# An MoE kernel: the last expert's products in high and low parts, and the gates' transposes in another place of the order

## Chip, core and metric

One core of one Trainium2 chip runs the whole program in one launch. The metric is the device time of an execution in microseconds (us); the kernel is run several times and the median is taken. One execution is also profiled: its span is the time from the first to the last instruction, and the profile's rows are measured from the span's start.

## What is computed

The program is a two-layer backbone over 256 latent tokens and 256 context tokens of width 1024 (fp32 everywhere): a recurrent mixer in layer 0, a short gated convolution in layer 1, and behind each a mixture of 16 experts, of which every token uses two. The change lies in the experts alone:

```python
combine = jnp.einsum('nk,nke->ne', gate, jax.nn.one_hot(experts, N_EXPERTS))
out = jnp.zeros_like(hf)
for e in range(N_EXPERTS):
    he = jax.nn.silu(hf @ w_gate[e]) * (hf @ w_up[e])     # 1024 -> 512, twice
    out = out + combine[:, e:e + 1] * (he @ w_down[e])    # 512 -> 1024
```

The reference computes every expert on every token; `combine` is zero where a token doesn't use the expert, so the kernel gathers only the tokens that do.

## The kernel before

`moe` runs once in each layer. The router gives each token its rank among the tokens of each of its experts. An expert has a fixed number of slots: 64 (`SL`) for experts 0 to 14, 128 for expert 15. If an expert got more tokens than slots, a branch behind expert 12 (`OVER`, the `If` at L1724) computes the rest; with this data the branch isn't taken, but every engine has to arrive at it.

What is done for one expert e, with the names of its tiles:

- **gather** (L1500, matmuls L1510, tile `xeps`): the columns of the normed tokens `h2t` are multiplied with a one-hot matrix `g`, for all experts of a group at once. The groups are experts 0-3, 4-7, 8-11, 12-14, and 15 alone; the gather of the next group is cut in four pieces, and one piece is issued in each iteration. ScalarE (L1519) and VectorE (L1516) evict the pieces into `xe`, with the layer's scale and shift.
- **gate_up** (L1548, matmuls L1558, tile `wup`): `xe` is the stationary operand, the weights `w` move through, 512 columns at a time. Eight blocks of the 1024 inputs, two matmuls each, for the gate and the up half. With 64 slots the two halves go to partitions 0-63 and 64-127, and the two matmuls of a block run side by side in the array. ScalarE (silu) and VectorE (product) make `sgate` of it.
- **turn** (L1566, transposes L1571, tile `hetp`): `sgate` is transposed; ScalarE copies it to `het`. It stands in the middle of the next expert's gate_up.
- **down** (L1576, matmuls L1585, tile `y`): four blocks, two matmuls each. ScalarE (L1596) and VectorE (L1597) evict `y` times the gate into `yy`, the one the positive part, the other what is left of it.
- **gates** (L1489, tile `gps`): two transposes of the one-hot matrix (L1493) and two one-column matmuls that pick the gate weights (L1495). ScalarE copies the transposes to `st` (L1497), VectorE the weights to `gw` (L1498).
- **scatter** (L1600, matmuls L1605, tile `acc`): `yy` is multiplied with `st` and added to the layer's output in PSUM.

In iteration e the program is written in the order gate_up(e), with turn(e - 1) in its middle; scatter(e - 2); down(e - 1); gates(e); one piece of the next group's gather. For expert 15 turn(14) stands ahead of its gate_up. A scheduler moves the instructions of an engine against each other within what their data allow, so the order on TensorE is not the written one.

All matmuls of gate_up and down are fp32, which TensorE executes as two passes: the trace has two rows for one such matmul. Gather and scatter are fp32r, a form with fewer bits that takes one pass. A layer's projections (L142 to L144, with the splits at L1105 and L1108) get fp32 accuracy with fp32r in another way: each operand is split in a high part (a cast to fp32r) and a low part (what is left), and three of the four products are added: high x high, low x high, high x low.

`gps`, `xeps` and `y` share a PSUM pool of two buffers (`psy`); `wup` and `hetp` have another. The weights come through a ring of eleven 1 MB tiles (`w`), six to an expert, on the queue of SyncE (L163): the next tile is asked for as soon as one is let go of.

Of the kernel before, what the change touches and what calls it, by code (L numbers as in the profile page):

```python
# [21 lines left out]
P = 128  # L22
# [107 lines left out]
class Kern:  # L130
# [1321 lines left out]
    def moe(self, l, h, ro, then):  # L1452
# [4 lines left out]
        with ExitStack() as outer:  # L1457
# [12 lines left out]
            pool = es.enter_context(tc.tile_pool(name="mo", bufs=2))  # L1470
            acc = [t[:, f] for t in [psa.tile([P, NB // 2, T], F32, name=f"acc{i}") for i in range(2)]
# [28 lines left out]
            def gather(g, ne, n, xe, step=2, turns=(psy, psy)):  # L1500

                m = ne * n
                for i in range(NB // step):
                    pl = turns[i % 2]
                    pt = pl.tile([P, 512], F32, tag="y" if pl is psy else "m", name="xeps")
                    for f in range(step):
                        fb = i * step + f
                        for j in range(4):
                            k, t = divmod(j, 2)
                            nc.tensor.matmul(pt[:, f * m:f * m + m], h2t[k][:, t, fb * P:fb * P + P],  # L1510
                                             g[:, t, :, :n], start=j == 0, stop=j == 3)
                    for f in range(step):
                        fb = i * step + f
                        src = pt[:, f * m:f * m + m].rearrange("p (e s) -> p e s", s=n)
                        if f % 2:
                            nc.vector.tensor_scalar(xe[:, fb], src, am[:, fb:fb + 1], bm[:, fb:fb + 1],  # L1516
                                                    op0=ALU.mult, op1=ALU.add)
                        else:
                            nc.scalar.activation(xe[:, fb], src, AF.Identity, bias=bm[:, fb:fb + 1],  # L1519
                                                 scale=am[:, fb:fb + 1])  # L1520
                    yield

            def again(src):

                def piece(k):
                    w = pool.tile([P, 1024], F32, tag="wov", name="wov")
# [20 lines left out]

            def gate_up(x, piece, after, tag=None, meanwhile=None):  # L1548

                n = x(0).shape[-1]  # L1550
# [12 lines left out]
                nc.vector.tensor_mul(sg, sg, gu[1])  # L1563
                return sg

            def turn(sg, tag=None):  # L1566
# [5 lines left out]
                het = pool.tile([P, 4, n], F32, tag=tag or f"het{n}", name="het", bufs=2 if n == SL and not tag else 1)  # L1572
                nc.scalar.copy(het, pt)
                return het

            def down(het, piece, gw, after, tags=("yy0", "yy1")):  # L1576


                n = het.shape[-1]
                ys = [psy.tile([P, 512], F32, tag="y", name="y") for _ in range(n // SL)]  # L1580
                ys = [ys[0][:SL], ys[0][SL:]] if n == SL else ys
                for k in range(4):
                    w = piece(k)
                    for i in range(2):
                        nc.tensor.matmul(ys[i], het[:, k], w[:, 512 * i:512 * i + 512], start=k == 0, stop=k == 3)  # L1585
                    after(k)
                if n == SL:
                    out = [[pool.tile([P, 512], F32R, tag=t, name="yy", bufs=2 if t[:2] == "yy" else 1)] for t in tags]
                    parts = [[out[i][0][SL * (i ^ q):SL * (i ^ q) + SL] for q in range(2)] for i in range(2)]
                    gws = [gw[:SL], gw[SL:]]  # L1590
                else:
                    parts = out = [[pool.tile([P, 512], F32R, tag=f"y{q}{i}", name="yy", bufs=1) for q in range(2)]
                                   for i in range(2)]
# [20 lines left out]
            def more(e):  # L1614

                with tc.If((over & (1 << e)) > 0):
# [6 lines left out]
                    het = turn(gate_up(lambda kc: xe[:, kc, 0], again(io["wgu"][l, e]), kept, "so0"), "heto")  # L1623
                    scatter(down(het, again(io["wd"][l, e]), gw, kept, ("so1", "ho")), st)

            def rest():

                with tc.If(most > 2 * SL):
# [12 lines left out]
                    for e in range(E):  # L1641
                        sgs = [pool.tile([P, FE], F32, tag=f"so{t}", name="so", bufs=1) for t in range(2)]
                        for i in range(2):
                            pts = [ps.tile([P, 512], F32, tag="m", name="wo_") for _ in range(2)]
                            for kc in range(NB):
                                w = pool.tile([P, 512], F32, tag="wov", name="wov2")
# [15 lines left out]
                        for i in range(2):  # L1662
                            pts = [psy.tile([P, 512], F32, tag="y", name="yps") for _ in range(2)]
                            for k in range(4):
                                w = pool.tile([P, 512], F32, tag="wov", name="wov2")
# [12 lines left out]
            def group(i, turns):  # L1678
# [3 lines left out]
                xe = pool.tile([P, NB, ne, n], F32, tag="xe", name="xe")  # L1682
                gx.append((g, xe))
                yield from gather(g, ne, n, xe, 2, turns)
# [16 lines left out]
            for e in range(E):  # L1701
# [4 lines left out]
                g, xe = gx[i]  # L1706
# [6 lines left out]
                new = gate_up(lambda kc: xe[:, kc, e - e0], ring(), release, None, meanwhile if n == SL else None)  # L1713
# [4 lines left out]
                sg, gate = new, gate_tiles()  # L1718
                gates(g, e - e0, e, *gate)
# [170 lines left out]
```

## Time and profile before

| | us |
|---|---|
| Median of three runs | 1366.07 |
| Lowest and highest of them | 1361.18, 1366.48 |
| The profiled execution | 1364.24 |
| Its span | 1362.4 |
| TensorE busy in the span | 1196.9 (88%) |
| VectorE busy | 763.2 (56%) |
| ScalarE busy | 582.8 (43%) |
| Weights and other reads from memory | 301.80 MB |

The two expert stages lie at about 690 to 954 us and 1088 to 1350 us. In a timeline of an engine a row is a run of equal instructions: start, duration, engine, line, operation, tiles, shape and count, and in brackets how long the engine stood idle ahead of it and what released it. Runs overlap a little, since matmuls are pipelined.

### The profile page before, as it was taken

To read this page: it belongs to the slowest core of one execution; us is meant where nothing else is said; L and a number is where in the kernel's file an instruction comes from. 1 tells how busy PE (TensorE), PEld (TensorE's weight loads), DVE (VectorE), ACT (ScalarE), POOL (GpSimd) and SP (SyncE) were. 2 spreads that over 40 slices of the span, in tenths; PEclk is the share of its full clock that TensorE was granted. 3 is DMA by queue.
4 is the path that set the end of the run, shared out by engine and by line. 5 is a ranking of instruction groups with operands and counts; after the bars stand their busy time and mean duration, and the time that the engine had idled before them with its cause. 6 is when DMAs were issued, how large, how long until landed. Compare 5 with 4: busy or idle time off the path is not lost. (4 is left out here: it accounts for less than half of the span.)

```text
span 1362.4 us, 22076 instructions
## 1 busy us (share of the span) xinstructions
PE 1196.9 (88%) x8560; PEld 845.6 (62%) x8560; DVE 763.2 (56%) x1855; ACT 582.8 (43%) x1187; POOL 235.4 (17%) x245
## 2 busy tenths in 40 slices
PE   2799888889989888899789999889898799999797
PEld 2588687777867777788744444334898734444344
DVE  5878888889989998875532121211677512121112
ACT  4667562666756757744312122212644312112113
POOL 3313443332231232100200000000523200000001
PEclk9999999999999999999889999989999899999898
DMA  9455634133322320137679999978653399999860
GB/s 355 177 178 172 211 109 124 59 121 115 96 90 83 96 82 25 64 138 315 227 295 418 420 420 419 419 296 324 214 186 129 119 376 419 419 420 420 326 245 31
DMA packets 64630, 311.76 MB, mean 229 GB/s; under 512 B 14464, under 2 KB 22912, under 8 KB 29696
## 3 DMA queue, kind: packets, MB, share of 16 engines
q1 hardware_dynamic: 60192, 303.59, 58.0%
q10 hardware_dynamic: 4320, 6.63, 1.4%
q8 instruction: 71, 1.16, 0.3%
q14 instruction: 47, 0.39, 0.1%
HBM read 301.80 MB, written 8.39 MB: 228 GB/s over the span
## 5 line engine op out<-in xcount | busy, mean ns | idle before, releaser
L1558 PE MATMUL wup<-w,xe 128*64 128x512 f32 (+1 forms) x1024 | 261.5, 612 | 5.8 <-DVEq L1724 5.8
L1563 DVE TENSOR_TENSOR sgate<-sgate,wup 64x512 f32<-64x512 f32 (+1 forms) x32 | 22.1, 690 | 250.1 <-ACT sgate L1562 227.6
L1558 PEld LDWEIGHTS wup<-w,xe 128*64 128x64 f32 (+1 forms) x1024 | 77.4, 142 | 129.6 <-issue 120.4
L1585 PE MATMUL y<-w,het 128*64 128x512 f32 (+1 forms) x512 | 127.7, 598 | 0.0
L1597 DVE SCALAR_TENSOR_TENSOR yy<-y,gw,yy 64x512 fp32r<-64x512 f32 (+1 forms) x64 | 48.0, 750 | 121.3 <-ACT yy L1596 121.0
L1562 ACT ACTIVATE sgate<-wup 64x512 f32<-64x512 f32 (+1 forms) x32 | 19.0, 593 | 181.6 <-PE wup L1558 181.6
L1596 ACT ACTIVATE yy<-y,gw 64x512 fp32r<-64x512 f32 (+1 forms) x64 | 43.8, 684 | 122.0 <-PE y L1585 106.5
L820 DVE TENSOR_TENSOR lv<-a_l,t_l 128x126 f32<-128x126 f32 (+22 forms) x248 | 81.7, 330 | 3.3
L822 DVE TENSOR_TENSOR t_l<-t_l,lv 128x126 f32<-128x126 f32 (+22 forms) x248 | 78.9, 318 | 3.4
L886 PE MATMUL po<-v_bd,hk 128*64 128x128 f32 (+1 forms) x256 | 56.6, 304 | 21.1 <-ACT s_bd L897 7.5
L1585 PEld LDWEIGHTS y<-w,het 128*64 128x64 f32 (+1 forms) x512 | 37.6, 140 | 60.5 <-issue 57.2
L1510 PEld LDWEIGHTS xeps<-g,h2t 128*128 128x128 f32 x256 | 37.5, 216 | 38.2 <-issue 21.3
L1510 PE MATMUL xeps<-g,h2t 128*128 128x256 f32 (+1 forms) x256 | 45.8, 321 | 17.2 <-DVE gw L1498 10.7
L1105 ACT CAST wh<-w 128x1024 fp32r<-128x1024 f32 x40 | 41.7, 1046 | 41.4 <-PE dps L143 24.3
L1771 POOL TENSOR_SCALAR idrw<-cst 128x1024 f32<-128x1024 f32 x2 | 5.5, 2770 | 303.0 <-PE acc L1605 274.0
L886 PEld LDWEIGHTS po<-v_bd,hk 128*64 128x64 f32 (+1 forms) x256 | 31.7, 163 | 41.3 <-ACT s_bd L897 14.4
L144 PE MATMUL dps<-xh,wl 128*128 128x258 f32 x192 | 55.2, 288 | 2.1 <-POOL wl L1108 2.1
L142 PE MATMUL dps<-xh,wh 128*128 128x258 f32 x192 | 55.5, 289 | 1.5 <-ACT wh L1105 1.5
L766 PE MATMUL pab<-bk,al_bd 128*128 128x128 f32 x256 | 40.4, 306 | 18.1 <-DVE bk L744 13.7
L722 POOL TENSOR_TENSOR al_bd<-kkh,peb 64x512 f32<-64x512 f32 x32 | 39.8, 1245 | 90.9 <-ACT peb L713 89.0
L1605 PE MATMUL acc<-st,yy 128*128 128x256 f32 x272 | 46.5, 305 | 10.3 <-PEq L1724 9.4
L143 PE MATMUL dps<-xl,wh 128*128 128x258 f32 x192 | 55.2, 287 | 0.0
(414 smaller groups left out, 2938.4 us busy)
## 6 DMA issues: line engine op xcount, KB each, us to landing
w<-in_wgu SPq DMA_DIRECT2D x128, 1024.0 KB, 9.6
w<-in_wd SPq DMA_DIRECT2D x64, 1024.0 KB, 9.4
w<-in_ada SPq DMA_DIRECT2D x46, 1024.0 KB, 6.5
w<-in_sc_in SPq DMA_DIRECT2D x12, 1024.0 KB, 5.0
w<-in_rk SPq DMA_DIRECT2D x8, 1024.0 KB, 5.3
w<-in_wv SPq DMA_DIRECT2D x4, 1024.0 KB, 5.8
w<-in_wo SPq DMA_DIRECT2D x4, 1024.0 KB, 9.3
w<-in_sc_out SPq DMA_DIRECT2D x4, 1024.0 KB, 5.2
```

Of the source, the lines that this page charges most:

```text
L142: mm(out, lhs[0], rhs[0], start=start, stop=False)
L143: mm(out, lhs[0], rhs[1], start=False, stop=False)
L144: mm(out, lhs[1], rhs[0], start=False, stop=stop)
L820: nc.vector.tensor_mul(u, a_l[:, kk:kk + 1, kk + 1:].broadcast_to([P, m, n]), t_l[:, 0:m, kk:kk + 1].broadcast_to([P, m, n]))
L822: nc.vector.tensor_sub(t_l[:, 0:m, kk + 1:], t_l[:, 0:m, kk + 1:], u)
L886: nc.tensor.matmul(po[d][i], q.hk[d][g][:, j], q.vbd[:, 4 * g + j], start=True, stop=i == 0)
L1510: nc.tensor.matmul(pt[:, f * m:f * m + m], h2t[k][:, t, fb * P:fb * P + P], g[:, t, :, :n], start=j == 0, stop=j == 3)
L1558: nc.tensor.matmul(gu[i], x(kc), w[:, 512 * i:512 * i + 512], start=kc == 0, stop=kc == NB - 1)
L1585: nc.tensor.matmul(ys[i], het[:, k], w[:, 512 * i:512 * i + 512], start=k == 0, stop=k == 3)
L1596: nc.scalar.activation(parts[i][0], ys[i], AF.Copy, scale=gws[i])
L1597: nc.vector.scalar_tensor_tensor(parts[i][1], ys[i], gws[i], parts[i][0].bitcast(F32), op0=ALU.mult, op1=ALU.subtract)
L1605: nc.tensor.matmul(acc[4 * i + q], part[:, q * P:q * P + P], st, start=first and q % 2 + k == 0, stop=last and k == len(y) - 1, skip_group ...
```

## The change

1. `gates(e)` is called right behind gate_up(e), ahead of scatter(e - 2) and down(e - 1), instead of behind them.
2. Expert 15 is computed with the three fp32r products. Its gather makes a scaled block `xt` (VectorE), casts it to `xh` (ScalarE) and subtracts to `xl` (VectorE); the new function `halves` does the same for each half tile of weights (`wh` on ScalarE, `wl` on VectorE, from a pool `ws` with two buffers each); the transposed activations are split into `het` and `hetl`. So gate_up has 48 matmuls there instead of 16 in two passes, and down 24 instead of 8. For the other experts `halves` issues the two matmuls as before.
3. To make room, `sg`, `yy` and the tiles of the branch have one buffer instead of two, and the four `yy` tiles of expert 15 share the memory of another tile.

```diff
-            def gather(g, ne, n, xe, step=2, turns=(psy, psy)):
+            def gather(g, ne, n, xe, step=2, turns=(psy, psy), low=None):
...
-                        if f % 2:
+                        if low is not None:
+                            t = pool.tile([P, n], F32, tag="xt", name="xt").unsqueeze(1)
+                            nc.vector.tensor_scalar(t, src, am[:, fb:fb + 1], bm[:, fb:fb + 1],
+                                                    op0=ALU.mult, op1=ALU.add)
+                            nc.scalar.copy(xe[:, fb], t)
+                            nc.vector.tensor_sub(low[:, fb], t, xe[:, fb].bitcast(F32))
+                        elif f % 2:
...
+            def halves(out, x, w, start, stop):
+
+                sets = [(x[0], w)]
+                if x[1] is not None:
+                    h, low = [ws.tile([P, 1024], F32R, tag=t, name=t) for t in ("wh", "wl")]
+                    nc.scalar.copy(h, w)
+                    nc.vector.tensor_sub(low, w, h.bitcast(F32))
+                    sets = [(x[0], h), (x[1], h), (x[0], low)]
+                for q, (a, b) in enumerate(sets):
+                    for i in range(2):
+                        nc.tensor.matmul(out[i], a, b[:, 512 * i:512 * i + 512], start=start and q == 0,
+                                         stop=stop and q == len(sets) - 1)
...
-                    for i in range(2):
-                        nc.tensor.matmul(gu[i], x(kc), w[:, 512 * i:512 * i + 512],
-                                         start=kc == 0, stop=kc == NB - 1)
+                    halves(gu, x(kc), w, kc == 0, kc == NB - 1)
                     after(kc)
-                sg = pool.tile([n, FE], F32, tag=tag or f"sg{n}", name="sgate", bufs=2 if n == SL and not tag else 1)
+                sg = pool.tile([n, FE], F32, tag=tag or "sg", name="sgate", bufs=1)
...
+                low = pool.tile([P, 4, n], F32R, tag="so1", name="hetl", bufs=1)
                 nc.scalar.copy(het, pt)
-                return het
+                nc.vector.tensor_sub(low, pt, het.bitcast(F32))
+                return het, low
...
-                    out = [[pool.tile([P, 512], F32R, tag=t, name="yy", bufs=2 if t[:2] == "yy" else 1)] for t in tags]
+                    out = [[pool.tile([P, 512], F32R, tag=t, name="yy", bufs=1)] for t in tags]
...
-                new = gate_up(lambda kc: xe[:, kc, e - e0], ring(), release, None, meanwhile if n == SL else None)
+                new = gate_up(lambda kc: [x if x is None else x[:, kc, e - e0] for x in xs], ring(), release, None, meanwhile if n == SL else None)
+                ngate = gate_tiles()
+                gates(g, e - e0, e, *ngate)
                 if outs:
                     scatter(*outs.pop(0))
                 for f in todo:
                     f()
-                sg, gate = new, gate_tiles()
-                gates(g, e - e0, e, *gate)
+                sg, gate = new, ngate
```

The order of TensorE's instructions changes throughout. The first place is among the first experts of layer 1; before, with y of one expert at the top and the next expert's first matmuls of gate_up (`wup`) around a gather piece:

```order
L1585 MATMUL y<-w,het 64x512 x8
L1493 MATMUL gps<-cst,g 128x128 x2
L1495 MATMUL gps<-r_cmb,g 128x1 x2
L1558 MATMUL wup<-w,xe 64x512 x3
L1510 MATMUL xeps<-g,h2t_13501 128x256 x2
L1510 MATMUL xeps<-g,h2t_13502 128x256 x2
L1510 MATMUL xeps<-g,h2t_13501 128x256 x2
L1510 MATMUL xeps<-g,h2t_13502 128x256 x2
L1558 MATMUL wup<-w,xe 64x512 x5
L1571 MATMUL hetp<-cst,sgate 128x64 x4
L1558 MATMUL wup<-w,xe 64x512 x8
L1605 MATMUL acc_14903<-st,yy 128x256 x4
```

and in the changed kernel, from y on:

```order
L1565 MATMUL y<-w,het 64x512 x8
L1511 MATMUL xeps<-g,h2t_13625 128x256 x2
L1511 MATMUL xeps<-g,h2t_13626 128x256 x2
L1511 MATMUL xeps<-g,h2t_13625 128x256 x2
L1511 MATMUL xeps<-g,h2t_13626 128x256 x2
L1565 MATMUL wup<-w,xe 64x512 x8
L1589 MATMUL hetp<-cst,sgate 128x64 x4
L1565 MATMUL wup<-w,xe 64x512 x8
L1494 MATMUL gps<-cst,g 128x128 x2
L1496 MATMUL gps<-r_cmb,g 128x1 x2
L1627 MATMUL acc_15030<-st,yy 128x256 x4
L1627 MATMUL acc_15031<-st,yy 128x256 x4
```

The gates (gps) have moved from behind y to ahead of the scatter, and the gather piece from behind the third matmul of gate_up to the front of all eight.

The second place is a few experts later in layer 1, where y itself is cut in two and the gather piece lies around its second half; before:

```order
L1585 MATMUL y<-w,het 64x512 x4
L1493 MATMUL gps<-cst,g 128x128 x2
L1495 MATMUL gps<-r_cmb,g 128x1 x2
L1510 MATMUL xeps<-g,h2t_13501 128x256 x2
L1510 MATMUL xeps<-g,h2t_13502 128x256 x2
L1510 MATMUL xeps<-g,h2t_13501 128x256
L1585 MATMUL y<-w,het 64x512 x4
L1510 MATMUL xeps<-g,h2t_13501 128x256
L1510 MATMUL xeps<-g,h2t_13502 128x256 x2
L1558 MATMUL wup<-w,xe 64x512 x4
L1571 MATMUL hetp<-cst,sgate 128x64 x4
```

and in the changed kernel:

```order
L1565 MATMUL y<-w,het 64x512 x4
L1511 MATMUL xeps<-g,h2t_13625 128x256 x2
L1511 MATMUL xeps<-g,h2t_13626 128x256 x2
L1511 MATMUL xeps<-g,h2t_13625 128x256 x2
L1511 MATMUL xeps<-g,h2t_13626 128x256 x2
L1565 MATMUL y<-w,het 64x512 x4
L1494 MATMUL gps<-cst,g 128x128 x2
L1496 MATMUL gps<-r_cmb,g 128x1 x2
L1565 MATMUL wup<-w,xe 64x512 x4
L1589 MATMUL hetp<-cst,sgate 128x64 x4
L1627 MATMUL acc_15030<-st,yy 128x256 x4
```

Before, gps stands between the halves of y with the gather behind it; now gps is behind the second half of y, with gate_up behind it.

The third place is ScalarE's order in the last expert of layer 1, from its sgate of expert 14 on; before:

```order
L1562 ACTIVATE sgate<-wup 64x512
L1497 CAST st<-gps 128x256
L1573 COPY het<-hetp 128x256
L1596 ACTIVATE yy<-y,gw 64x512
L1519 ACTIVATE xe<-xeps,mod_73,modam_13574 128x128
L1596 ACTIVATE yy<-y,gw 64x512
L1519 ACTIVATE xe<-xeps,mod_73,modam_13574 128x128
L1562 ACTIVATE sgate<-wup 128x512
L1596 ACTIVATE yy<-y,gw 64x512
```

and in the changed kernel:

```order
L1580 ACTIVATE sgate<-wup 64x512
L1618 ACTIVATE yy<-y,gw 64x512
L1592 COPY het<-hetp 128x256
L1520 CAST xh<-xt 128x128 x2
L1560 CAST wh<-w 128x1024
L1618 ACTIVATE yy<-y,gw 64x512
L1560 CAST wh<-w 128x1024 x2
L1520 CAST xh<-xt 128x128 x2
L1498 CAST st<-gps 128x256
L1560 CAST wh<-w 128x1024 x5
```

Casts of `w` and of `xt` stand now between the evictions of expert 13 (the first two yy), the gates of expert 15 (st) and the silu of expert 15 (sgate).

## Rows read from the trace of the kernel before

**Rows 1.** Busy time by engine, expert stage of layer 1: length, PE, PEld, DVE, ACT, POOL, clock, DMA share, GB/s.
```profile
1160.00:1180.00 20.00, 19.35 (x99) 7.96 (x100) 2.89 (x5) 3.15 (x6) 0.00 (x0) 1.00 1.01 419
```

**Rows 2.** Timeline of TensorE, an expert with y cut in two, layer 1.
```profile
1166.95 0.44 PE L1493 MATMUL gps<-cst,g 128*128 128x128 f32 x2
...
1168.38 0.85 PE L1510 MATMUL xeps<-g,h2t 128*128 128x256 f32 x5 [0.65 <-DVE gw L1498]
1169.16 1.94 PE L1585 MATMUL y<-w,het 128*64 128x512 f32 x8
...
1173.83 1.21 PE L1605 MATMUL acc<-st,yy 128*128 128x256 f32 x8
...
1183.42 0.85 PE L1510 MATMUL xeps<-g,h2t 128*128 128x256 f32 x5 [0.65 <-DVE gw L1498]
```

**Rows 3.** Timeline of TensorE, one of the first experts of layer 1.
```profile
1123.39 0.44 PE L1493 MATMUL gps<-cst,g 128*128 128x128 f32 x2
...
1124.09 1.93 PE L1558 MATMUL wup<-w,xe 128*64 128x512 f32 x6
...
1127.09 2.79 PE L1558 MATMUL wup<-w,xe 128*64 128x512 f32 x10
```

**Rows 4.** Timeline of TensorE, scatter of an expert with a 192-wide gather, layer 1.
```profile
1234.29 0.73 PE L1605 MATMUL acc<-st,yy 128*128 128x256 f32 x4
...
1236.82 0.75 PE L1605 MATMUL acc<-st,yy 128*128 128x256 f32 x4
```

**Rows 5.** Weight tiles from issue to landing, first at 1110 to 1125, then 1260 to 1275 us.
```profile
DMA to landing us min/median/max: 10.9/12.0/13.0
DMA to landing us min/median/max: 8.5/9.1/10.0
```

**Rows 6.** Timeline of TensorE behind the branch of layer 1.
```profile
1286.18 4.53 PE L1558 MATMUL wup<-w,xe 128*64 128x512 f32 x10 [3.17 <-DVEq L1724]
```

**Rows 7.** Timeline of TensorE, the last two experts of layer 1.
```profile
1316.04 0.55 PE L1510 MATMUL xeps<-gl,h2t 128*128 128x128 f32 x3 [0.26 <-DVE gw L1498]
...
1321.61 12.23 PE L1558 MATMUL wup<-w,xe 128*128 128x512 f32 x28
1333.28 1.52 PE L1605 MATMUL acc<-st,yy 128*128 128x256 f32 x8
...
1340.01 0.74 PE L1605 MATMUL acc<-st,yy 128*128 128x256 f32 x4 [0.42 <-DVE yy L1597]
```

**Rows 8.** Durations: line groups (ns min/median/max), then timeline rows of ScalarE, VectorE, TensorE.
```profile
L1105 ACT CAST wh<-w x40: 1032/1049/1053, 628.9 to 1057.1; 128x1024 fp32r<-128x1024 f32 x40
L1108 DVE TENSOR_TENSOR wl<-w,wh x27: 1214/1225/1239, 629.9 to 1054.9; 128x1024 fp32r<-128x1024 f32 x27
1338.49 0.68 ACT L1596 ACTIVATE yy<-y,gw 64x512 fp32r<-64x512 f32 x1 [4.87 <-PE y L1585]
1339.20 0.75 DVE L1597 SCALAR_TENSOR_TENSOR yy<-y,gw,yy 64x512 fp32r<-64x512 f32 x1 [4.57 <-ACT yy L1596]
1322.31 0.41 DVE L1516 TENSOR_SCALAR xe<-xeps,modam,mod 128x128 f32<-128x128 f32 x1 [0.83 <-ACT xe L1519]
98.11 0.40 PE L142 MATMUL lps<-x,wh 128*128 128x512 f32 x1
98.34 0.39 PE L143 MATMUL lps<-x,wh 128*128 128x512 f32 x1
```

**Rows 9.** Three windows as in rows 1; then who waited for L1105, L1108 (us, times).
```profile
954.00:958.00 4.00, 2.52 (x70) 2.12 (x69) 4.00 (x10) 3.45 (x9) 3.34 (x2) 1.00 0.88 291
958.00:961.00 3.00, 0.88 (x6) 0.68 (x7) 3.00 (x5) 3.00 (x9) 3.00 (x3) 0.98 0.97 410
961.00:964.00 3.00, 3.00 (x16) 3.00 (x16) 2.97 (x7) 0.72 (x3) 2.92 (x4) 0.50 0.47 197
  PE dps L142: 1.5, 1
  PE dps L144: 3.4, 2
```

More of the change, by code (lines that the diff above doesn't have):

```diff
@@ L1470, in moe @@
             pool = es.enter_context(tc.tile_pool(name="mo", bufs=2))
+            ws = es.enter_context(tc.tile_pool(name="mows", bufs=2))
             acc = [t[:, f] for t in [psa.tile([P, NB // 2, T], F32, name=f"acc{i}") for i in range(2)]
@@ L1525, in piece @@
                 def piece(k):
-                    w = pool.tile([P, 1024], F32, tag="wov", name="wov")
+                    w = pool.tile([P, 1024], F32, tag="wov", name="wov", bufs=1)
                     nc.gpsimd.dma_start(w, src[:, k * 1024:k * 1024 + 1024])
@@ L1583, in down @@
                     w = piece(k)
-                    for i in range(2):
-                        nc.tensor.matmul(ys[i], het[:, k], w[:, 512 * i:512 * i + 512], start=k == 0, stop=k == 3)
+                    halves(ys, [x if x is None else x[:, k] for x in het], w, k == 0, k == 3)
                     after(k)
                 if n == SL:
-                    out = [[pool.tile([P, 512], F32R, tag=t, name="yy", bufs=2 if t[:2] == "yy" else 1)] for t in tags]
+                    out = [[pool.tile([P, 512], F32R, tag=t, name="yy", bufs=1)] for t in tags]
                     parts = [[out[i][0][SL * (i ^ q):SL * (i ^ q) + SL] for q in range(2)] for i in range(2)]
@@ L1591, in down @@
                 else:
-                    parts = out = [[pool.tile([P, 512], F32R, tag=f"y{q}{i}", name="yy", bufs=1) for q in range(2)]
-                                   for i in range(2)]
+                    y4 = pool.tile([P, 4, 512], F32R, tag="xa", name="yy", bufs=1)
+                    parts = out = [[y4[:, 2 * i + q] for q in range(2)] for i in range(2)]
                     gws = [gw, gw]
@@ L1622, in more @@
                     gates(g, 0, e, gw, st)
-                    het = turn(gate_up(lambda kc: xe[:, kc, 0], again(io["wgu"][l, e]), kept, "so0"), "heto")
+                    het = turn(gate_up(lambda kc: (xe[:, kc, 0], None), again(io["wgu"][l, e]), kept, "so0"), "heto")
                     scatter(down(het, again(io["wd"][l, e]), gw, kept, ("so1", "ho")), st)
@@ L1645, in rest @@
                             for kc in range(NB):
-                                w = pool.tile([P, 512], F32, tag="wov", name="wov2")
+                                w = pool.tile([P, 512], F32, tag="wov", name="wov2", bufs=1)
                                 nc.gpsimd.dma_start(w, io["wgu"][l, e][:, kc * 1024 + i * 512:kc * 1024 + i * 512 + 512])
@@ L1664, in rest @@
                             for k in range(4):
-                                w = pool.tile([P, 512], F32, tag="wov", name="wov2")
+                                w = pool.tile([P, 512], F32, tag="wov", name="wov2", bufs=1)
                                 nc.gpsimd.dma_start(w, io["wd"][l, e][:, k * 1024 + i * 512:k * 1024 + i * 512 + 512])
@@ L1681, in group @@
                 g = onehot(e0, ne, 0, "g" if n == SL else "gl", n == SL)
-                xe = pool.tile([P, NB, ne, n], F32, tag="xe", name="xe")
-                gx.append((g, xe))
-                yield from gather(g, ne, n, xe, 2, turns)
+                if n == SL:
+                    xe, low = pool.tile([P, NB, ne, n], F32, tag="xe", name="xe"), None
+                else:
+                    xe, low = [pool.tile([P, NB, ne, n], F32R, tag=t, name=t, bufs=1) for t in ("xh", "xl")]
+                gx.append((g, xe, low))
+                yield from gather(g, ne, n, xe, 2, turns, low)
             gx = []
```

11 lines of the change are left out of this document (7 added, 4 removed).

## The prediction

> **What bounds the kernel now.** I read the profile by stage first: the whole-span share of TensorE is an average over a mixer, a router and two expert stages, and only the last two are touched. The expert stage runs from about 690 to 954 us in layer 0 and 1088 to 1350 us in layer 1. In a steady stretch of it [rows 1] TensorE is busy 19.35 of 20 us, VectorE 2.89, ScalarE 3.15, and the DMA share is 1.01 at 419 GB/s. So TensorE sets the pace, and the weight stream runs at its ceiling right behind it; which of the two ends later must be settled before a gain on TensorE is believed.
>
> Then I read TensorE's own timeline for one expert. Nine times a layer, one expert of some 15 us apart (two neighbours stand at 1168.38 and 1183.42 us), it stands still .65 us at the gather piece, released by VectorE's eviction gw of the gates' tile: the one-hot transposes (gps) are followed directly by the gather (xeps), and both take their PSUM from the same two-buffer pool [rows 2]. From the start of gps to the next matmul is 1.43 us there, against .70 us where gate_up follows gps [rows 3]. Each such place costs .73 us.
>
> Next, the expert's 512-column fp32 matmuls run in pairs, one in each half of the array (each such matmul is two rows of the trace). Three times a layer the gather is put after three of eight matmuls of gate_up, an odd number, which leaves a matmul without its partner: 6 rows take as long as 8 (1.93 against 1.94 us), and the ten behind take 2.79 [rows 2, 3]. So 1.93 + 2.79 = 4.72 us against 2 x 1.94 = 3.88: .84 us for each broken pair.
>
> In the group whose gather is 192 wide (four experts a layer) the scatter is cut in two by gate_up. Its two halves take .73 + .75 us against 1.21 whole [rows 2, 4]: .27, of which some .07 is the end of the second run, which overlaps what follows.
>
> The weight stream: 6.29 MB an expert at 419 GB/s is 15.01 us. Eleven 1 MB tiles, six to an expert, mean that a tile is issued some ten tiles, 10 x 15.04 / 6 = 25 us, before it is used; it lands 12.0 us (13.0 at most) after its issue early in layer 1 and 9.1 late in it [rows 5]. So 12 us of slack stand at the start, and the queue is catching up, not falling behind.
>
> **The change part by part.** It moves gates(e) ahead of scatter and down of expert e - 1, splits the last expert's operands, and reduces buffer counts.
>
> *Gates.* In the new order gps stands behind the second half of down and is followed by gate_up, which needs neither gw nor that PSUM pool; the gather then follows y matmuls. Gain 9 x .73 = 6.6 us a layer, **13.1** in both. It rests on the .70 us of [rows 3], where the same two neighbours stand. Lower bound 0, if the gather finds another eviction late; the two-buffer pool now hands it the buffer of the y two turns back, evicted an expert ago, so I take it whole.
>
> *Pairs.* The order keeps all eight matmuls together in each of the three places: 3 x .84 = 2.5, **5.1** in both layers; bounds 0 and 5.1, since no place loses more than these rows show.
>
> *Scatter in one piece.* .20 each, eight times: **1.6**; bounds 0 and 2.2 (.27 each).
>
> *New waits in the middle.* Where the pattern changes, once a layer, the scatter follows the evictions of its second half more closely. The bounds are 0 and one ScalarE plus one VectorE eviction, .68 + .75 [rows 8]; I take .85, near the VectorE one, on which it waits last: **-1.7**. At the branch behind expert 12 TensorE waits 3.17 us for VectorE to arrive [rows 6]. VectorE now has four operations for the first gather piece of expert 15 (a scaling and a subtraction for each of two blocks) where it had one, and one scaling went to ScalarE. At .41 each [rows 8] the four make 1.6 a layer; the scalings run while TensorE is still at the same piece, so I take the two subtractions, .8: **-1.6** in both (bounds 0 and -3.3).
>
> *The last expert.* A 128 x 128 x 512 fp32 matmul is two rows; 28 rows take 11.67 us from start to start [rows 7], .417 each. The sixteen of gate_up are 32 x .417 = 13.3 us and the eight of down 6.7. In fp32r one takes .23 (98.11 to 98.34, [rows 8]), three products make 48 x .23 = 11.0 and 24 x .23 = 5.5. TensorE saves 2.3 + 1.15 = 3.45 us a layer. Against that stand waits, since each piece needs a cast on ScalarE (1.05) and then a subtraction on VectorE (1.23, [rows 8]) ahead of its third product. Twelve pieces are 12.6 and 14.8 us against 16.5 on TensorE: they fit, but only just, and the first of each stage is not hidden. Ahead of gate_up I count: gates(14) behind the gather's evictions 1.1, the last gather piece .7, the first cast .7 (ScalarE has an eviction and two casts of xh ahead of it), the first subtraction .35: 2.9. In down: scatter(14) waits 1.5 instead of .42, since its yy evictions queue behind the casts; casts .28 + .23 + .17 and subtractions .81 + .35; and the last eviction .7 instead of .1, since both output halves now end together: 3.5 more than before. Gone are a .65 and a .26 us wait in the two experts before (1.0 with the restart). Net 2.9 + 3.5 - 1.0 - 3.45 = 2.0 a layer slower: **-3.9** in both. These are the least certain numbers, worked out from order and durations and not read; bounds -1 (waits hidden by work that runs ahead) and +4 a layer.
>
> For the pace of such splits the trace has a precedent: in the layer's own projection 40 pieces are split the same way, and TensorE's products of it waited once for a cast, 1.5 us, and twice for subtractions, 3.4 [rows 9]. That supports a wait at the start rather than one at each piece.
>
> *The rest.* Fewer buffers for sg and yy: both are rewritten an expert (14 us) later and are read within 3 us, so nothing; if a yy were late it would cost the 1.43 of its two evictions. SP issues the same tiles in the same order: nothing. Dropped branch code isn't run.
>
> **Sum:** 13.1 + 5.1 + 1.6 - 1.7 - 1.6 - 3.9 = 12.6 us. The profiled execution took 1364.24 (span 1362.4 and 1.8 around it) and would take 1351.6; the median before is 1366.07, 1.83 above it, so **1353.4**, said as 1353.
>
> **Rivals.** A measurement of this kernel can tell about .5%, 6.8 us, from no change: faster means under 1359.2, slower over 1372.9.
>
> *TensorE's clock drops to its lower level in the last expert.* For it: at the start of that projection in layer 1 TensorE was busy .88 of 3 us and then ran at a granted .50, the 1.2 GHz level, for 3 us [rows 9]. Against: a stretch busy 2.52 of 4 us kept 1.00 [rows 9], and the last expert as I count it is busy 16.6 of about 23 us. At the lower level each product costs .23 more; down alone 24 x .23 = 5.5 us a layer. One layer gives 1359, both 1364. The Trainium skill, in "TensorE: Matmul & The Clock Gate", section "A second HAM failure mode: psum-queue depth-cycling", describes a kernel whose clock oscillated because TensorE idled briefly and often between groups of matmuls, which is this shape. By that rule the time is the 1364. The rows show the drop only behind longer idling: chance .12.
>
> *The weight stream becomes the bound.* TensorE would consume an expert in 14.3 us against 15.0 of supply; over thirteen experts up to the branch it eats 13 x .7 = 9 of the 12 us of slack, and at the branch the stream catches up for 7 us. If a third of that slack isn't there (other traffic, later landing), 3 us a layer are lost: 1359; if none, 9: 1371. For it: the share of 1.01. Against: 13.0 us to land, falling to 9 [rows 5]. Chance .09.
>
> *The splits run in series with the products (the slower side).* With two buffers for wh and wl, ScalarE may only start on a piece when TensorE has let go of an earlier one. Cast and subtraction in series, 2.28 us a piece, make 12 x 2.28 = 27.3 against my 16.5 + 6.4 = 22.9: 4.4 a layer, 1362. Cast, subtraction and six products (1.38) in series make 3.66 x 12 = 43.9: 21 a layer, 1395. The kernel gets slower than before from 22.9 + 6.3 over 12, 2.43 us a piece, and measurably from 2.7. For it: the last expert's yy and gate evictions share both engines. Against: the precedent above. Chance .07, .05 of it beyond 1372.9.
>
> *The gates' move does nothing:* the gather finds another late eviction (st on ScalarE or a y). Then 13.1 are missing: 1366.5, no change. Chance .06.
>
> **How the numbers follow.** Forecast .66, and the four rivals .12, .09, .07, .06. Faster: .66, with those halves of the clock and of the stream that end under 1359.2 (.06 + .05): .77. Slower: .05 of the splits and .02 of the stream (no slack at all, with the last expert at its upper bound): .07. Same: .16. The range: my own low end is 1353.4 with the last expert at -1 (5.9), the middle waits at 0 (3.3): 1344, rounded to 1345; upward it takes in the last expert at +4 (4.0) and the clock's and half of the stream's cases: 1362.
>
> **What would show it right or wrong.** Right: no row of xeps that waits for gw; steady experts of 14.2 to 14.4 us; wup always in runs of eight rows or more around a gather; DMA share at 1.0 and no TensorE wait on tile w; in the last expert waits on wh and wl at the first piece only, and a stage some 2 us longer. Wrong: a granted clock near .5 after 1320 us; waits on w from about the tenth expert; a wait on wl in front of every third product; xeps waiting as before for another name.

## The result and the profile after

The changed kernel takes 1347.65 us (median of four runs, 1346.82 to 1348.97) against 1365.62 for the kernel before beside it: a ratio of 0.9884, 95% interval 0.986 to 0.9909. The forecast was 1353 in a range of 1345 to 1362, so the time lies in the range, 5 us below the forecast.

The profiled execution has a span of 1346.2 us (1347.99 in all). Cut at points that both traces have, its 16.2 us come from here. "Experts" runs from the first gate_up matmul to the last y ahead of the branch, "branch" from that y to the next gate_up matmul, "rest" from there to the next stage's first matmul. The last two columns are experiments that are told below.

| us | before | changed | gates only (e1) | split only (e2) |
|---|---|---|---|---|
| up to the first gate_up, layer 0 | 693.70 | 693.69 | 696.22 | 692.94 |
| experts, layer 0 | 185.84 | 174.41 | 174.41 | 185.84 |
| branch, layer 0 | 10.69 | 11.90 | 11.75 | 12.27 |
| rest, layer 0 | 67.64 | 69.52 | 67.62 | 69.06 |
| mixer and router, layer 1 | 131.62 | 133.00 | 132.31 | 134.43 |
| experts, layer 1 | 185.85 | 174.41 | 174.40 | 185.84 |
| branch, layer 1 | 10.84 | 11.56 | 11.31 | 11.09 |
| rest, layer 1 | 65.73 | 66.99 | 65.68 | 67.37 |
| end | 10.49 | 10.72 | 10.30 | 9.56 |
| span | 1362.4 | 1346.2 | 1344.0 | 1368.4 |

The experts up to the branch got 11.4 us shorter in each layer, 22.9 in all. Everything else got longer: the branch 1.9, the rest 3.1, the mixer behind layer 0 1.4, the end .2.

Timeline of TensorE in the changed kernel, one of the first experts of layer 1, where [rows 3] showed the pair that was broken (start, duration, line, tiles, shape, count):

```profile
1098.58 3.65 PE L1565 MATMUL y<-w,het 128*64 128x512 f32 x16
1102.17 1.21 PE L1511 MATMUL xeps<-g,h2t 128*128 128x256 f32 x8
1103.31 3.65 PE L1565 MATMUL wup<-w,xe 128*64 128x512 f32 x16
1106.89 0.46 PE L1589 MATMUL hetp<-cst,sgate 64*128 64x64 f32 x4
...
1112.62 3.65 PE L1565 MATMUL y<-w,het 128*64 128x512 f32 x16
```

The sixteen rows of gate_up stand in one run of 3.58 us (1103.31 to 1106.89), and an expert takes 14.04 us (y to y).

The expert with y cut in two, the counterpart of [rows 2]; the last row is the second of the two y of the expert behind:

```profile
1168.92 1.89 PE L1565 MATMUL y<-w,het 128*64 128x512 f32 x8
1170.73 1.19 PE L1511 MATMUL xeps<-g,h2t 128*128 128x256 f32 x8
1171.86 1.94 PE L1565 MATMUL y<-w,het 128*64 128x512 f32 x8
1173.72 0.44 PE L1494 MATMUL gps<-cst,g 128*128 128x128 f32 x2
...
1174.43 1.94 PE L1565 MATMUL wup<-w,xe 128*64 128x512 f32 x8
1176.30 0.46 PE L1589 MATMUL hetp<-cst,sgate 64*128 64x64 f32 x4
1176.69 0.73 PE L1627 MATMUL acc<-st,yy 128*128 128x256 f32 x4
1177.62 0.73 PE L1627 MATMUL acc<-st,yy 128*128 128x256 f32 x4 [0.20 <-DVE yy L1619]
...
1186.43 1.94 PE L1565 MATMUL y<-w,het 128*64 128x512 f32 x8
```

No gather piece waits for gw any more, and the piece is whole. From gps to gate_up it is .71 us. One new wait of .20 stands in each layer, at the scatter. From y to y an expert of this kind takes 14.57 us here and 14.11 where the scatter doesn't wait.

The last two experts of layer 1, the counterpart of [rows 7]:

```profile
1286.69 0.30 PE L1494 MATMUL gps<-cst,g 128*128 128x128 f32 x1 [0.92 <-DVE xt L1518]
...
1301.89 1.08 PE L1511 MATMUL xeps<-gl,h2t 128*128 128x128 f32 x8 [0.53 <-DVE xt L1518]
1303.17 0.72 PE L1565 MATMUL wup<-wh,xh 128*128 128x512 f32 x2 [0.20 <-ACT wh L1560]
...
1322.30 0.74 PE L1627 MATMUL acc<-st,yy 128*128 128x256 f32 x4 [1.20 <-DVE yy L1619]
...
1324.19 0.51 PE L1565 MATMUL y<-wl,het 128*128 128x512 f32 x1 [0.53 <-DVE wl L1561]
...
1328.08 0.62 PE L1565 MATMUL y<-wh,hetl 128*128 128x512 f32 x2
1328.77 0.73 PE L1565 MATMUL y<-wl,het 128*128 128x512 f32 x2
...
1331.45 2.25 PE L1627 MATMUL acc<-st,yy 128*128 128x256 f32 x16 [0.54 <-ACT yy L1618]
```

The six rows with a bracket are all the waits that the timeline lists there, 3.9 us; layer 0 has the same six. Between them stand shorter gaps that it doesn't list: two products take .47 us from start to start at the usual pace, and .69 ahead of the last row for wl (1328.08 to 1328.77). The windows of that stretch (length, PE, PEld, DVE, ACT, POOL, granted clock, DMA share, GB/s) show the clock at its upper level in this execution, and VectorE and ScalarE busy for most of the first:

```profile
1300.00:1316.00 16.00, 15.19 (x77) 11.62 (x74) 13.46 (x19) 10.97 (x16) 0.00 (x0) 1.00 0.04 16
1316.00:1332.00 16.00, 13.65 (x59) 7.31 (x57) 8.20 (x9) 7.70 (x10) 0.00 (x0) 1.00 0.00 0
```

Behind the last expert of layer 0, the next projection's first cast and first subtraction come later; before, the two waits were 1.48 and 2.12 us:

```profile
949.52 0.39 PE L142 MATMUL dps<-xh,wh 128*128 128x258 f32 x1 [2.75 <-ACT wh L1105]
...
952.98 0.58 PE L144 MATMUL dps<-xh,wl 128*128 128x258 f32 x1 [2.96 <-POOL wl L1108]
```

The weight stream no longer keeps up with TensorE. From issue to landing (us, min/median/max), tiles issued at 1100 to 1115 and at 1247 to 1262 us of the changed kernel, against [rows 5]:

```profile
DMA to landing us min/median/max: 10.6/11.5/12.6
DMA to landing us min/median/max: 18.8/20.2/20.9
```

TensorE didn't wait for a weight tile in the stretch, but its lead (the time by which a tile lands ahead of its use) shrank by 8.7 us within ten experts.

### The profile page after: what moved, and what is told of

Read it like the earlier page. It is cut to its first block, busy times and chain, and to the rows that moved or that the text cites. A ratio compares the mean times of both kernels' runs of the same rounds, so it can differ in the third digit from the quotient of the medians.

```text
span 1346.2 us, 22273 instructions
## 1 busy us (share of the span) xinstructions
PE 1181.9 (88%) x8608; PEld 851.1 (63%) x8608; DVE 799.9 (59%) x1905; ACT 606.2 (45%) x1219; POOL 234.3 (17%) x245
## 5 line engine op out<-in xcount | busy, mean ns | idle before, releaser
L1565 PE MATMUL wup<-w,xe 128*64 128x512 f32 x960 | 224.7, 611 | 8.7 <-DVEq L1750 8.7
L1565 PEld LDWEIGHTS wup<-w,xe 128*64 128x64 f32 x960 | 65.4, 139 | 121.4 <-issue 114.6
L1565 PE MATMUL y<-w,het 128*64 128x512 f32 x480 | 113.9, 599 | 0.0
L1565 PEld LDWEIGHTS y<-w,het 128*64 128x64 f32 x480 | 31.5, 136 | 53.2 <-issue 49.1
L1105 ACT CAST wh<-w 128x1024 fp32r<-128x1024 f32 x40 | 41.7, 1046 | 45.0 <-PE dps L143 28.0
L1627 PE MATMUL acc<-st,yy 128*128 128x256 f32 x272 | 42.3, 294 | 13.3 <-PEq L1750 9.5
L142 PE MATMUL pps<-x,wh 128*128 128x512 f32 (+1 forms) x128 | 43.6, 361 | 10.4 <-ACT x L361 8.8
```

The costliest lines, as they stand in the source:

```text
L142: mm(out, lhs[0], rhs[0], start=start, stop=False)
L1105: self.nc.scalar.copy(h, w)
L1565: nc.tensor.matmul(out[i], a, b[:, 512 * i:512 * i + 512], start=start and q == 0, stop=stop and q == len(sets) - 1)
L1627: nc.tensor.matmul(acc[4 * i + q], part[:, q * P:q * P + P], st, start=first and q % 2 + k == 0, stop=last and k == len(y) - 1, skip_group ...
```

## The experiments

Up to the first gate_up two executions of the same kernel differ by 1.4 us (e1 and e6, 696.22 and 694.82) and 2.1 (the changed kernel and e5, 693.69 and 691.62), so the stretches of the traces carry the readings below, and the medians where several executions were taken on one chip.

**One part alone: the gates (e1).** The edit in the kernel before:

```diff
+                ngate = gate_tiles()
+                gates(g, e - e0, e, *ngate)
                 if outs:
                     scatter(*outs.pop(0))
                 for f in todo:
                     f()
-                sg, gate = new, gate_tiles()
-                gates(g, e - e0, e, *gate)
+                sg, gate = new, ngate
```

> The kernel before with the gates moved and nothing else: the last expert stays fp32, all buffer counts stay. Theory A (the two traces): the stretch of experts up to the branch gets 11.8 us a layer shorter by the move alone, and the split of the last expert is a loss, so this gives back 2 x 11.8 and the two waits behind the branch, 1365.6 - 25 = about 1340, and the branch's wait for VectorE falls back from 4.5 to 3.2 us. Theory B (the terms of the prediction: 19.8 us for the gates): 1346. Theory C (part of the gain comes from the split or from the buffer counts): 1348 or more, slower than the changed kernel.

1345.91 us against 1363.14, ratio 0.9887 (0.9855 to 0.9919). The stretch of experts is the changed kernel's to a hundredth: 174.41 and 174.40. So all of the 22.9 us is the move's, and the split has no part in it. The time is the one that theory B gave, but B's gain for the gates, 19.8, is not what the stretches show. The rest of the expert stage is at 67.62 and 65.68, as before the change. The branch is at 11.75 and 11.31, though its last expert is fp32: that half of theory A fell.

**The other part alone: the split (e2).** The changed kernel with the edit of e1 undone.

> The changed kernel with the gates back behind down: only the high and low parts of the last expert and the buffer counts are left. Theory A (traces): a loss of 1.3 us at the branch and 2 to 3 us in the last expert and behind it, each layer: 1365.6 + 8 = 1372 to 1375. Theory B (the prediction's sum: 1.6 for the branch, 3.9 for the last expert): 1371. Theory C (the TensorE time that the three products save, 3.45 us a layer, arrives at the end): 1359.

1367.46 us, ratio 1.0044 (1.0021 to 1.0068): slower than before by .4%, as A and B have it, by less than both. The experts are at 185.84 in both layers. The rest is 1.4 and 1.6 us longer, the mixer behind layer 0 2.8.

**The cause of the order, with the gates left in place (e3).** One line of the kernel before:

```diff
-                pt = psy.tile([P, 512], F32, tag="y", name="gps")
+                pt = ps.tile([P, 512], F32, tag="m", name="gps")
```

> The kernel before with one line changed: the tile of the gates (gps) comes from the PSUM pool of gate_up and the transposes instead of the pool of gather and down. The written order stays, gates behind down. If the shared two-buffer pool is what cut the pairs, the gather and the scatter into pieces (theory A), the order repairs itself without the move, and it gains nearly what the move gains: 20 to 25 us, 1341 to 1346. If only the .65 us waits hang on the pool (theory B) it gains 13: 1352. If gps now delays gate_up or the transposes, which share two buffers with it (theory C), it is near 1366.

1348.35 us, ratio 0.991 (0.9875 to 0.9944). The experts take 177.90 and 177.93 us: 7.9 of the 11.4 us a layer come without the move. The broken pairs and the waits for gw are gone, so it is the shared pool of two buffers that made both. The rest is missing since gps now splits gate_up itself, and the scatter waits. Its timeline of TensorE in layer 0:

```profile
774.47 0.75 PE L1605 MATMUL acc<-st,yy 128*128 128x256 f32 x4 [0.36 <-DVE yy L1597]
775.06 0.38 PE L1493 MATMUL gps<-cst,g 128*128 128x128 f32 x2
775.37 1.94 PE L1558 MATMUL wup<-w,xe 128*64 128x512 f32 x8
777.24 0.61 PE L1495 MATMUL gps<-r_cmb,g 128*128 128x1 f32 x4
777.77 3.65 PE L1558 MATMUL wup<-w,xe 128*64 128x512 f32 x16
```

**The chain ahead of the last expert (e4).** One line of the changed kernel:

```diff
-                            nc.scalar.copy(xe[:, fb], t)
+                            nc.scalar.activation(xe[:, fb], src, AF.Identity, bias=bm[:, fb:fb + 1],
+                                                 scale=am[:, fb:fb + 1])
```

> The changed kernel with one line changed: ScalarE makes xh straight from the PSUM tile (scale, shift and cast in one), beside VectorE's xt, instead of a cast behind xt. The chain ahead of a free PSUM buffer gets shorter by nothing on VectorE (two xt of .41 us each still stand ahead of the next gather piece) but the subtraction can no longer stand between them. If the .92 and .53 us waits for xt in the last two experts are the order of VectorE's queue, they go: 1.4 us a layer, 1345; if they are the two scalings alone, nothing changes: 1348. The branch's wait for VectorE should stay at 4.2 to 4.6 us, since VectorE has the same four operations there.

1349.07 us (1343.03 to 1350.17), not told apart from the changed kernel. The waits for xt went, as expected, but most of what they cost came back at the scatters: from the first hetp behind the branch to the last run of the scatter, layer 0 takes 56.08 us against 56.46 in the changed kernel, .4 less where 1.4 was expected. Layer 1 takes 57.34, since TensorE's clock fell there (see the rivals below). Its timeline of TensorE, layer 1:

```profile
1289.15 0.44 PE L1494 MATMUL gps<-cst,g 128*128 128x128 f32 x2 [0.30 <-ACT xh L1520]
...
1302.42 0.73 PE L1628 MATMUL acc<-st,yy 128*128 128x256 f32 x4 [0.98 <-DVE yy L1620]
1322.71 0.74 PE L1628 MATMUL acc<-st,yy 128*128 128x256 f32 x4 [0.98 <-DVE yy L1620]
```

**Both on one chip (e5, e6).** The changed kernel and the kernel of e1 again, six executions of each.

> The changed kernel once more, beside e6 on the same chip. By the stages of the traces (from the first gate_up matmul to the branch, the branch, the rest of the expert stage) the split of the last expert costs 3.6 us in both layers and .7 in the projection behind layer 0. Then this is 4 us slower than e6. If the .9 us step between the medians of e1 and the changed kernel is all, it is 1 to 2 us slower; if the split is worth its TensorE time, it is faster than e6.

> The gates moved and nothing else, as in e1, for the comparison with e5 on one chip. By the stages 4 us faster than e5, at 1342 to 1346, and 21 us faster than the kernel before.

1345.33 us (1342.88 to 1349.96) with the split, ratio 0.9884 (0.9854 to 0.9914); 1340.25 (1336.2 to 1341.86) without it, ratio 0.9833 (0.9805 to 0.9861). The version with the gates alone is 5.1 us faster by the medians, and its six runs all lie below the other's. It is the fastest kernel of this study. In the two traces the rest and the mixer are 2.1 + .2 + 2.8 = 5.1 us longer with the split. Of the 2.8, in layer 1, 1.2 is a fall of TensorE's clock in the last expert of e5, which the changed kernel's first trace doesn't have (see the rivals below).

**The weight stream as the next bound (e7, e8).** One number in the changed kernel and in the kernel before:

```diff
-NRING = 9
+NRING = 5
```

> The changed kernel with four 1 MB weight tiles fewer (a ring of 7 instead of 11). In the trace of the changed kernel a tile lands 11.5 us after its issue at the start of the stage and 20.9 at its end, with some 23.5 between issue and use: an expert takes 14.1 us and the stream 15.0. Four tiles fewer take 9.4 us of lead away. If the lead was nearly used up (theory A), TensorE now waits for w in the last experts ahead of the branch, and the stretch up to the branch grows from 174.4 by 3 to 6 us a layer, with rows that wait for DMA w. If the stream isn't close to binding (theory B), the stretch stays within 1 us of 174.4. The branch tells something more: it took 10.7 us before and 11.3 to 11.9 with the gates moved; if a deep queue of weights delays what the branch fetches, it falls back to 10.8.

> The kernel before with the same ring of 7 tiles. There an expert takes 15.04 to 15.31 us against the stream's 15.0, so the lead of the start stays. Theory A and B both: no TensorE wait for w of more than .5 us, the stretch up to the branch stays at 185.8 or gets up to 1.7 us shorter where the order keeps more pairs together. If it grows by 3 us or more as well, the smaller ring costs something by itself, and e7 tells nothing of the change.

The kernel before keeps its 186.19 us in both layers, with no wait for a tile, and tiles that land in 8.1 to 9.6 us at the end. The changed kernel goes from 174.41 to 179.52 and 179.35, and waits for a wd tile five times a layer. Timeline of TensorE in e7, layer 0, and its landing times at 1247 to 1262 us:

```profile
804.96 1.94 PE L1565 MATMUL y<-w,het 128*64 128x512 f32 x8 [0.42 <-DMA w<-in_wd]
819.91 1.94 PE L1565 MATMUL y<-w,het 128*64 128x512 f32 x8 [0.58 <-DMA w<-in_wd]
834.87 1.94 PE L1565 MATMUL y<-w,het 128*64 128x512 f32 x8 [0.60 <-DMA w<-in_wd]
849.84 1.94 PE L1565 MATMUL y<-w,het 128*64 128x512 f32 x8 [0.60 <-DMA w<-in_wd]
```
```profile
DMA to landing us min/median/max: 13.9/15.3/16.9
```

The rows are 14.95 to 14.97 us apart: the stream's 15.0 sets the pace from the eighth expert on. Theory A holds. The ring of eleven tiles is what lets the gain through. The branch, at 11.92 and 11.52, didn't fall back in e7; in e8 it is at 10.28 and 10.42, .4 below the kernel before.

**What the split costs, by taking most of it away (e9, first edit) and by taking it from down (e10, second edit).** Both start from the changed kernel. The first leaves eleven of the twelve splits out of the computation.

```diff
-                    h, low = [ws.tile([P, 1024], F32R, tag=t, name=t) for t in ("wh", "wl")]
-                    nc.scalar.copy(h, w)
-                    nc.vector.tensor_sub(low, w, h.bitcast(F32))
+                    if not cut:
+                        cut.extend(ws.tile([P, 1024], F32R, tag=t, name=t, bufs=1) for t in ("wh", "wl"))
+                        nc.scalar.copy(cut[0], w)
+                        nc.vector.tensor_sub(cut[1], w, cut[0].bitcast(F32))
+                    h, low = cut
```
```diff
-                low = pool.tile([P, 4, n], F32R, tag="so1", name="hetl", bufs=1)
                 nc.scalar.copy(het, pt)
-                nc.vector.tensor_sub(low, pt, het.bitcast(F32))
-                return het, low
+                return het, None
```

> The changed kernel, but only the first of the twelve weight pieces of expert 15 is split; the other eleven are left out of the computation and the products of all pieces use the parts of the first. TensorE does the same 72 products; eleven casts and eleven subtractions are gone. The stretch behind the branch is 67.6 and 65.7 us with fp32 (before, e1) and 69.5 and 67.0 in the changed kernel. If the loss is the splitting work and the waits for it (theory A), the products' 3.45 us a layer arrive, less the two waits for xt (1.4): 65.6 and 63.7, and the wait for the first cast of the next projection falls from 2.75 back to 1.48. If the loss comes from elsewhere, the gather's longer chain and the order (theory B), it stays within 1 us of 69.5 and 67.0.

> The changed kernel with the down part of expert 15 back in fp32: four of the twelve pieces are not split, gate_up keeps its three products. Down gets 1.15 us longer on TensorE, and loses the waits for wl (.53), for the last eviction (.54 beside .1) and part of the wait for yy (1.20 to .42). By that the stretch behind the branch gets .6 us shorter in layer 1 (66.4), and in layer 0 1.9 shorter (67.6), since ScalarE is free earlier for the next projection's cast. If the waits of down were not the splits', it gets 1.15 longer: 70.7 and 68.1.

One profile each. The cleanest stretch is from the first hetp behind the branch to the last run of the scatter: 55.35 and 55.37 us before, 55.25 and 55.24 with the gates alone, 56.46 and 56.48 in the changed kernel, 54.66 in both layers of e9, 55.01 and 55.00 in e10. The second trace of the changed kernel, e5, has 56.46 and 57.65, the latter with the fall of the clock.

So without eleven of the twelve splits the stretch gets 1.8 us shorter, and still saves only .6 of the 3.45 us that TensorE's products save against e1. Behind the work of splitting, the chain of small steps stays; e9's timeline of TensorE, layer 1:

```profile
1285.24 0.30 PE L1494 MATMUL gps<-cst,g 128*128 128x128 f32 x1 [0.91 <-DVE xt L1518]
...
1300.43 1.08 PE L1511 MATMUL xeps<-gl,h2t 128*128 128x128 f32 x8 [0.53 <-DVE xt L1518]
...
1320.54 0.50 PE L1569 MATMUL y<-wh,het 128*128 128x512 f32 x1 [0.94 <-ACT het L1599]
1328.19 2.24 PE L1631 MATMUL acc<-st,yy 128*128 128x256 f32 x16 [0.54 <-ACT yy L1622]
```

Both theories hold a part: the stage and what follows up to the next matmuls is at 68.40 and 65.17 in e9, between A's 65.6 and 63.7 and B's 69.5 and 67.0. In e10 the split of gate_up alone is worth .24 us a layer against e1; splitting down costs 1.47 on top. Up to the next matmuls e10 has 71.38 and 65.34, where 67.6 and 66.4 were expected. The whole of it, 1350.53 us, says nothing of the splits: in layer 0 the next projection's first matmuls came in another order, with an idle time of 4.74 us. The wait for that projection's first cast didn't fall back in e9 either (3.54 us, expected 1.48). The traces show what sets it: the order on ScalarE. From its first operation for the projection to that cast it is 2.24 us and seven operations before, 3.52 and nine in the changed kernel, 4.31 and eleven in e9, and the differences, 1.28 and 2.07, are those of the waits. Why the scheduler orders them so stays open. The whole of e9 took 1343.97.

## Why the prediction was right, and where its terms were off

**What bounds the kernel, and the move's mechanism: right.** No wait for gw is left, the pairs and the scatter are whole, and all of the gain is in the stretch in which it was forecast; e1 shows that it is the move's, and e3 that the shared two-buffer pool was the cause.

**The size of that gain: under-estimated**, 19.8 less 1.7 for the new waits, against 22.9 measured. By kind of expert, a layer:

- Three with a broken pair: 15.12 to 14.02-14.04 us, 1.1 each, where .84 was forecast. The step that failed was the yardstick: two runs of eight at 1.94 by duration. The whole run takes 3.58 by starts, and before, 1.87 + 2.72 = 4.59 by starts: 1.01, and 6.1 in both layers, over the bound of 5.1. Adding durations of two pipelined runs counts the overlap of their ends twice. The two runs of [rows 3] end where these rows of the kernel before start:

```profile
1125.96 1.21 PE L1510 MATMUL xeps<-g,h2t 128*128 128x256 f32 x8
...
1129.81 0.46 PE L1571 MATMUL hetp<-cst,sgate 64*128 64x64 f32 x4
```

- Four with y cut and a 256-wide piece: 15.04 to 14.11, .93 each, where .73 was forecast. Missed was that the gather piece itself was cut by y: .78 us ahead of y [rows 2] and .55 behind it, against 1.13 in one run. The second half, before:

```profile
1171.03 0.62 PE L1510 MATMUL xeps<-g,h2t 128*128 128x256 f32 x3
1171.58 0.65 PE L1558 MATMUL wup<-w,xe 128*64 128x512 f32 x2
```

- Four with a 192-wide piece: 15.31 to 14.14, 1.17 each, where .73 + .20 was forecast. By starts, gps gave back .80, the scatter .21 and the unbroken 24 rows of gate_up .15, which the working left out.
- The new wait, .20 by the timeline, costs .46 once a layer (14.57 against 14.11), where .85 was taken between 0 and 1.43.

3 x 1.1 + 4 x .93 + 4 x 1.17 - .46 = 11.2; the last .2 is at the expert ahead of the branch.

**The branch: right in size (1.9 for 1.6) by luck, wrong in cause.** The term was VectorE's added operations. VectorE ends only .24 us later, counted from the last y (5.25 against 5.01 us), and e1, whose VectorE has the same work there as before, has 1.06 and .47 of it. From VectorE's last operation to the next gate_up it is 5.7 and 5.8 us before and 6.1 to 6.7 in e1 and e6. What lengthens it isn't shown. In e3, which has neither the move nor the split, the branch is at 11.71 and 11.26 too. For the depth of the weight queue as the cause the runs speak both ways: with four tiles fewer the branch keeps its length in e7 and loses .4 in e8.

**The last expert: right in sign, and about in size by luck.** Forecast 3.9 us of loss in both layers. By e1 against the changed kernel the rest and the mixer behind it lose 1.90 + 1.31 + .69 = 3.9, by e6 against e5 5.1. Within the stage it is 1.2 a layer, not 2.0. The listed waits ahead of gate_up are 1.65, where 2.9 was counted, and in down 2.3, where 4.0 was. Against that, the products saved less than 2.3 + 1.15. By starts, without the runs between them and the listed waits, those of gate_up take 11.8 us (13.1 before), and those of down 7.0 (6.55 before, and 5.9 in e9, which has no splits there): the gaps that the timeline doesn't list took all of down's saving. What else was missed lies behind the stage: 1.05 us in layer 0 up to the next projection's first matmul, since ScalarE has two more operations ahead of its cast (see e9), and .84 more at its first subtraction. The sum met the forecast because errors of both signs cancel.

**The rivals.** In the profiled execution of the result the clock stayed at 1.00 through the last expert, with TensorE busy 13.65 of 16 us. In other traces it did not. Seven traces have the split, two layers each, and in three of the fourteen last experts the clock fell to its lower level for some 3 us: e5 in layer 1, e4 in layer 1, e7 in layer 0. Each time it cost 1.2 to 1.3 us from the first hetp behind the branch to the scatter, where the rival took 5.5. None of the ten last experts in fp32 has such a fall. Window and timeline of e5, with the same kernel as the result; two products take .82 us from start to start instead of .47:

```profile
1300.00:1304.00 4.00, 4.00 (x15) 2.89 (x13) 3.93 (x8) 2.67 (x5) 0.00 (x0) 0.57 0.01 2
1300.18 1.03 PE L1565 MATMUL wup<-wh,xl 128*128 128x512 f32 x2
1301.00 1.09 PE L1565 MATMUL wup<-wl,xh 128*128 128x512 f32 x2
```

The waits ahead of it are .92, .53 and .20 us, those of the result's execution, where it didn't fall; what decides isn't shown. So the rival's mechanism was there in some executions, at less than a quarter of its price. The rule named with that rival, in the Trainium skill's "TensorE: Matmul & The Clock Gate", section "A second HAM failure mode: psum-queue depth-cycling", is borne out by these three last experts and not by the other eleven; no run here shows more of it.

The splits didn't run in series: after the first piece no product waits for a wl in gate_up. The weight stream was the rival that came closest: 9 of 12 us of lead were to go by the working, 8.7 went, and e7 shows the loss when the lead is missing.

**The range and the sum.** 12.6 us forecast, 16.2 in the traces: the terms of the gates were 4.8 short, and the losses 1.1 short (5.5 forecast, 6.6 measured: 1.9, 3.1, 1.4, .2). The medians are 18.0 apart; of the 1.8 between that and the traces nothing is shown but the spread of the executions, 5.3 us in the kernel before.

## What to carry to other kernels

When small steps borrow from a pool of two buffers that a long chain also uses, look at what the scheduler does around the wait and not only at the wait: here the nine idle times of .65 us were half of the price, 5.9 of 11.4 us a layer, and the rest was runs cut into pieces. Price a cut by the start of a run to the start of what follows, with the whole run as yardstick, not by adding durations. Fewer products on the bounding engine can be worth nothing where they need casts and subtractions in a chain that ends in the eviction: here, of 3.45 us a layer nothing arrived, and the change is better without that half. Look for a fall of the clock in more than one trace: the result's own showed none, its repeat did. And before trusting a gain under a saturated stream, count the lead in tiles: here eleven carried it, seven don't.

## What the runs showed of the hardware

Behind the branch TensorE runs at its lower level (1.2 of 2.4 GHz), after 8 to 9 us in which it had one matmul of the scatter to do. The window behind the branch in layer 1 has a granted clock of .50 before and .54 in the changed kernel (first and second row), and the first run of gate_up takes 6.5 us there instead of 3.6.

```profile
1284.00:1292.00 8.00, 5.82 (x14) 1.90 (x16) 0.00 (x0) 0.00 (x0) 0.00 (x0) 0.50 0.22 52
```
```profile
1268.00:1275.00 7.00, 6.51 (x17) 1.98 (x17) 0.00 (x0) 0.00 (x0) 0.00 (x0) 0.54 1.01 415
```

What that costs differs between executions of the same kernel. The first row is e1, the second e6, TensorE's timeline, the same run of sixteen rows in layer 1:

```profile
1268.02 6.64 PE L1558 MATMUL wup<-w,xe 128*64 128x512 f32 x16 [4.46 <-DVEq L1725]
```
```profile
1266.47 5.01 PE L1558 MATMUL wup<-w,xe 128*64 128x512 f32 x16 [4.22 <-DVEq L1725]
```

That is 1.6 us in which nothing of the kernel differs. The program's start is the other such place (692 to 698 us up to the first gate_up with the ring of eleven tiles). The two make 3.0 of the 3.9 us between the traces of e1 and e6, while the stretch of experts between them agrees to hundredths. The medians of e1 and e6 differ by 5.7 us, though the kernel before took 1363.14 and 1362.88 beside them; what makes the rest isn't shown.

In the changed kernel's order an early rise and the later fall went together. In the three layers with a fall in the last expert the first run of gate_up behind the branch took 5.0 to 5.6 us by starts; in the other eleven with the split it took 6.05 to 6.5, but for one with 5.3 (e2, layer 0), which has the gates in their old place. That is three cases, and no run shows the reason.
